# LayerNorm tail of a hybrid decoder layer: all norms on VectorE, the half-filled token tile first in the last column block, one thread per store

## The chip, the cores and the metric

The kernel runs on one core of a Trainium2 chip. The core has five engines that work side by side, each through its own instruction stream: TensorE (PE, matrix products into PSUM), VectorE (DVE), ScalarE (ACT), GpSimd (POOL) and SyncE (SP, which here issues every DMA). The metric is the device time of one execution in microseconds (us), the median of several runs. The profile is of one execution; its "span" is the time from the first to the last recorded instruction of the core.

## The reference, cut to what matters

One layer of a hybrid decoder step: a combined input projection, an RWKV-7 branch and a retention branch, an output projection, and a post-norm. It is done for 16 + 512 tokens of a new sequence and for 64 tokens of eight running sequences, all with 2048 features in float32. The change touches only the end:

```
h = jnp.einsum('btc,cd->btd', jnp.concatenate([o_a, o_b], axis=-1), w_out)
y = _layer_norm(ALPHA * x + h, ln_g, ln_b)
# _layer_norm: (x - mean) * rsqrt(var + 1e-5) * g + b, over the 2048 features of a token
```

The 512 prompt tokens and the 64 sample tokens are 576 rows of output: four tiles of 128 tokens (t = 0 to 3) and one of 64 (t = 4, the half-filled tile).

## The kernel before, in words

**The order of the work.** No engine's instruction stream is written out by hand. A class `Order` records the work as Python generators ("jobs"); each has a priority (`od.start(name, generator, priority)`, a small number goes first). While the main loop issues matmuls, `pump` puts in what the jobs have ready; when the main loop must wait, or has ended, `force` issues the job operation that can start first by the planner's own clock, with a penalty of `FIRST` = 200 per priority step once the matmuls are through. `od.call` defers a piece of Python until the operations ahead of it in the job are issued. What results is one fixed stream per engine. Each stream runs in order: an instruction whose inputs are not there holds up all that stand behind it on its engine. Since every operation passes through helpers, all DVE, ACT and POOL instructions carry line L363 in the profile, the matmuls L386 and the DMAs L403.

**The output projection.** The 2048 output columns are cut into four blocks of 512 (n = 0 to 3), and the 2048 inputs into 16 chunks of 128 (ki). A "cell" (n, t) is one 128 x 512 tile of the product, built in one of eight PSUM banks in turn (`obank`). Products are made from values split into a high and a low part: three matmuls per chunk for t < 4 and two for t = 4, whose matmul with the 64 low rows of the activations fills the upper half of the same bank. A weight chunk is loaded by DMA, and ACT and DVE split it into `wh` and `wl` (`gen_split`). For n = 3 the last ten chunks are held in SBUF (`HELD`): the tile that comes first in the order takes them as they come, and the other tiles follow, one whole tile after the other. In the kernel before, that order is t = 0, 1, 2, 3, 4.

**After a cell** (`gen_cell`): DVE adds ALPHA * x (loaded by `gen_xin` into one of three buffers, in the order of the cells) to the bank and writes `hh`, part of the tile named RW in the profile; for t = 4 a second DVE operation adds the upper half of the bank. Then `bn_stats` of the 512 columns. After the last cell of a token tile, `gen_stat` makes mean and variance (`bn_aggr`, tile SHT) and POOL makes rstd = (var + 1e-5)^-0.5 in two operations on one column.

**The norm** (`gen_norm`) of a token tile goes over four pieces of 512 columns. A string `SHARE` has a letter for each piece, four per token tile. For "g" (t = 0 to 2, and columns 0 to 1023 of t = 3) there are three steps on three engines: ACT computes x * rstd + nm, with nm = -mean * rstd made by DVE in one small operation; DVE multiplies by ln_g; POOL adds ln_b. For "d" (the rest of t = 3, all of t = 4) there are two DVE operations: (x - mean) * ln_g, and (that) * rstd + ln_b. Each piece's store to DRAM is issued by the same job, behind the piece's last step.

Of the kernel before, what the change touches and what calls it, by code (L numbers as in the profile page):

```python
# [12 lines left out]
ACTF = mybir.ActivationFunctionType  # L13
ALU = mybir.AluOpType
# [25 lines left out]
NPRIO = 1  # L40
OPRIO = 1
FIRST = 200.0
SHARE = "ggggggggggggggdddddd"
LATE = 5
EARLY = 14
BACKLOG = {0: 4000.0, 1: 1000.0, 2: 500.0, 3: 300.0, 4: 100.0}
# [360 lines left out]
def kernel(ctx, tc, x_prompt, x_sample, state_rwkv, state_shift, state_ret, meta_tokens, w_in, w_out,  # L407
# [3 lines left out]
    od = Order()  # L411
    V, A, G = (Engine(e, k, od) for e, k in ((nc.vector, "DVE"), (nc.scalar, "ACT"), (nc.gpsimd, "POOL")))
    T = TensorEngine(nc.tensor, od)
    mm = T.matmul
    S = Dma(nc.sync, "SP", od)
    S2 = Dma(nc.scalar, "AQ", od)
    until, mark, stage = od.until, od.mark, od.stage
# [40 lines left out]
    NM = sht[:, 120:125]  # L458
    RSTD = sht[:, 135:140]
    MV = sht[:, 125:135].rearrange("p (a b) -> p a b", b=2)  # L460
# [94 lines left out]
    def act(out, in_, func=ACTF.Copy, scale=1.0, bias=0.0):  # L555
        A.activation(out=out, in_=in_, func=func, scale=scale, bias=bias)

    def tt(out, a, b, op=ALU.mult, e=None):
        (e or V).tensor_tensor(out=out, in0=a, in1=b, op=op)

    def stt(out, a, s, b, o0=ALU.mult, o1=ALU.mult, e=None):
        (e or V).scalar_tensor_tensor(out=out, in0=a, scalar=s, in1=b, op0=o0, op1=o1)

    def ts(out, a, s1, s2=None, o0=ALU.mult, o1=ALU.add, e=None):
        if s2 is None:
            (e or V).tensor_scalar(out=out, in0=a, scalar1=s1, scalar2=None, op0=o0)
        else:
            (e or V).tensor_scalar(out=out, in0=a, scalar1=s1, scalar2=s2, op0=o0, op1=o1)
# [432 lines left out]
    def span(u, half):  # L1001

        if half:
            return H0, H1
        t0 = {"A": 14 * (u[2] in "rg"), "B": 16 * (u[2] in "qg"), "L": 0}[u[0]]
        return t0, H0 - t0
# [74 lines left out]
    chunks = []  # L1081
    events = []
# [8 lines left out]
    korder = [i for p in range(NPAIR) for i in ((p, 8 + p) if p < NPAIR - 1 else (8 + p, p))]  # L1091
    KO = len(korder)
    tiles = range(5)
    cells = [(n, t) for n in range(4) for t in tiles]
    j_in = len(chunks)
    for i in range(EARLY):
        events.append(("out", len(chunks), 0, i, (0, 1)))
        chunks.append(("out", korder[i], 0))
    for n in range(4):
        for i in range(KO):  # L1100
            events.append(("out", len(chunks), n, i, (2, 3, 4) if n == 0 and i < EARLY else tiles))
            chunks.append(("out", korder[i], n))
    j_one = j_in + EARLY + KO
    last = {ev[1]: e for e, ev in enumerate(events)}
# [48 lines left out]
    with tc.manual_schedule():  # L1153
# [78 lines left out]
        hh = RW[:, 0:10240].rearrange("p (t n) -> p t n", t=5)  # L1232
        lng = RW[:, 10240:12288]
        lnb = RW[:, 12288:14336]
        xin = [RW[:, 14336 + 512 * i:14336 + 512 * i + 512] for i in range(3)]
        obank = [(sq, pj[0], pj[1], r0, r1, m0, m1, ob)[i % 8] for i in range(len(cells))]
# [47 lines left out]
        def gen_stat(t):  # L1284
            rows = trows(t)
            mv = MV[0:rows, t, :]
            V.bn_aggr(out=mv, in_=ST6[0:rows, t].rearrange("p a b -> p (a b)"))
            rs = RSTD[0:rows, t:t + 1]
            ts(rs, mv[:, 1:2], 1.0, 1e-5, e=G)
            tt(rs, rs, NEGH[0:rows, 0:1], ALU.pow, e=G)  # L1290
            nm = NM[0:rows, t:t + 1]
            if set(SHARE[4 * t:4 * t + 4]) != {"d"}:
                stt(nm, mv[:, 0:1], -1.0, rs)
            od.call(lambda: od.start(f"N{t}", gen_norm(t), NPRIO))
            yield

        def gen_norm(t):
            rows = trows(t)
            rs, nm, mu = RSTD[0:rows, t:t + 1], NM[0:rows, t:t + 1], MV[0:rows, t, 0:1]
            dst = y_prompt[0, 128 * t:128 * t + 128, :] if t < 4 else xsamp_y  # L1300
            for n, step in ((0, 0), (1, 0), (0, 1), (2, 0), (1, 1), (0, 2), (3, 0), (2, 1), (1, 2), (3, 1), (2, 2), (3, 2)):
                sl = slice(512 * n, 512 * n + 512)
                hw = hh[0:rows, t, sl]
                who = SHARE[4 * t + n]
                if who == "d":
                    if step == 0:
                        stt(hw, hw, mu, lng[0:rows, sl], ALU.subtract, ALU.mult)
                    elif step == 2:
                        stt(hw, hw, rs, lnb[0:rows, sl], ALU.mult, ALU.add)
                elif step == 0:  # L1310
                    act(hw, hw, ACTF.Identity, rs, nm)
                elif step == 1:
                    tt(hw, hw, lng[0:rows, sl])
                else:
                    tt(hw, hw, lnb[0:rows, sl], ALU.add, e=G if who == "g" else V)
                if step == 2:
                    S.dma_start(out=dst[:, sl], in_=hw)
            yield

        xsamp_y = y_sample.rearrange("b t d -> (b t) d")  # L1320
# [24 lines left out]
        late = []  # L1345
        for e, ev in enumerate(events):
            stage["event"] = e
            j = ev[1]
            if ev[0] == "in":
                _, j, u, half, q, ui = ev  # L1350
                kind, p, s = u
                if half == 0 and q == 0:
                    if kind == "A" and s == "k":
                        od.start(f"A{p}", gen_a(p), 1)
                    if kind == "B" and s == "q":
                        od.start(f"B{p}", gen_b(p), 3)
                if q == 0 and ui:
                    od.ensure("evac", 2 * ui - 1 + half)
                if ui == 0 and half == 1 and q == 0:
                    od.ensure("x", 99)  # L1360
                od.ensure("split", j + 1)
                t0, n = span(u, half)
                b, jb = pj[half], part[j]
                for kk in range(4):
                    kt = 4 * q + kk
                    w = slice(128 * kk, 128 * kk + 128)
                    for i, (a_, x_) in enumerate(((WH[jb], xh), (WH[jb], xl), (WL[jb], xh))):
                        mm(b[:, :n], a_[:, w], x_[:, kt, t0:t0 + n], start=(kt == 0 and i == 0), stop=(kt == 15 and i == 2))
                        if kk == 3 and i == 2:
                            stage["event"] = e + 1  # L1370
                            if q == 3:
                                stage["proj"] = 2 * ui + half + 1
                        od.pump()
            else:
                _, j, n, ki, some = ev
                od.ensure("o", ki + 1)
                if ki == 0:
                    if n == 0 and 4 in some:
                        od.ensure(f"B{NPAIR-1}", 99)
                        od.ensure("shift", 99)  # L1380
                    if n:
                        od.ensure(f"F{NPAIR-1}", 99)
                        od.ensure("cell", 5 * n + 5 - 8)
                od.ensure("split", j + 1)
                work = [(t, ki, part[j]) for t in some]
                if n == 3 and ki >= KO - HELD:
                    late += work[1:]
                    work = work[:1]
                    if ki == KO - 1:
                        work += sorted(late, key=lambda w: w[0])  # L1390
                for iw, (t, k_, jb) in enumerate(work):
                    b = obank[5 * n + t]
                    if k_ == 0 and b in pj:
                        od.ensure("evac", 2 * len(units) - 1 + pj.index(b))
                    tok = slice(128 * t, 128 * t + 128)
                    if t < 4:
                        todo = [(b, xo[:, k_, tok], WH[jb]), (b, xl[:, k_, tok], WH[jb]), (b, xo[:, k_, tok], WL[jb])]
                    else:
                        todo = [(b, xo[:, k_, tok], WH[jb]), (b[0:64], xo[:, k_, 512:576], WL[jb])]
                        if k_ == KO - 1:  # L1400
                            todo.reverse()
                    for i, (b_, x_, w_) in enumerate(todo):
                        end = i == len(todo) - 1
                        mm(b_, x_, w_, start=(k_ == 0 and i == 0), stop=(k_ == KO - 1 and end))
                        if k_ == KO - 1 and end:
                            stage["out"] = 5 * n + t + 1
                        if iw == len(work) - 1 and end:
                            stage["event"] = e + 1
                        od.pump()
# [41 lines left out]
```

## Time and profile before

| | us |
|---|---|
| median of the runs (lowest to highest) | 1382.36 (1382.06 to 1383.02) |
| the profiled execution | 1382.55 |
| its span | 1380.8 |
| PE busy | 1331.4 (96%) |
| DVE busy | 884.0 (64%) |
| ACT busy | 644.7 (47%) |
| POOL busy | 72.5 (5%) |

The profiled execution took 1.75 us more than its span and 0.19 us more than the median. The mean granted TensorE clock was 0.991. Busy shares are means over the whole span; the change lies in the last 60 us, so what is read are the rows of that stretch: start, duration, engine, operation, output<-inputs, and in brackets the idle time before it and what ended it. The last matmul of the kernel starts at 1356.81 us; the remaining 24 us of the span have no TensorE work.

### The profile page before, as it was taken

The numbers are of one execution on the slowest core, as the hardware profiler recorded it, in microseconds if no ns is written. First come the engines' busy times: TensorE is split into PE (matmuls) and PEld (weight loads), VectorE is DVE, ScalarE is ACT, GpSimd is POOL, SyncE is SP. The second block draws the span as 40 slices with busy tenths as digits, with TensorE's granted clock in tenths as the row PEclk, the third lists the DMA queues.
The fourth block names the chain that finished last, engine by engine and source line by source line (L and its number), as shares of the span: only waits on it lengthen the run. The fifth ranks groups of instructions, "written<-read, shape, count | busy, mean of one in ns | idle before, by whom it ended". The sixth has DMA issues, their size and how long they took to land.

```text
span 1380.8 us, 26964 instructions
## 1 busy us (share of the span) xinstructions
PE 1331.4 (96%) x10392; PEld 1230.1 (89%) x10392; DVE 884.0 (64%) x2158; ACT 644.7 (47%) x1519; POOL 72.5 (5%) x131
## 2 busy tenths in 40 slices
PE   7999999999999999999999999999999999999993
PEld 6999899989998999899989998999899987777782
DVE  5774677566766676667666765676567658624347
ACT  4534564366336633663356435643564366512121
POOL 0000000000000000000000000100010001000024
PEclk9999999999999999999999999999999999999997
DMA  7343224322432243224322432243224347654313
GB/s 238 87 109 90 69 74 118 94 66 72 118 87 73 66 123 85 75 65 120 84 81 64 118 80 81 63 118 85 80 62 120 88 138 214 195 166 117 98 48 122
DMA packets 232342, 139.79 MB, mean 101 GB/s; under 512 B 58668, under 2 KB 212102, under 8 KB 231238
## 3 DMA queue, kind: packets, MB, share of 16 engines
q1 hardware_dynamic: 232214, 138.08, 35.3%
q8 instruction: 81, 1.33, 0.4%
q14 instruction: 47, 0.39, 0.1%
HBM read 119.30 MB, written 18.74 MB: 100 GB/s over the span
## 4 chain that ended last, share of the span: by engine, by line
PE 81%; DVE 9%; ACT 6%; issue 3%; DMA 0%; POOL 0%; DVEq 0%; SPq 0%; ACTq 0%; POOLq 0%
PE bank L386 77%; DVE RW L363 5%; PE bank L392 4%; DVE wl L363 1%; ACT RW L363 1%; ACT SF L363 1%; ACT XH L363 1%; DVE MOM L363 1%; ACT RT L363 1%; ACT RHS L363 1%; ACT wh L363 1%; DVE RT L363 1%; ACT RSv L363 1%; DVE SHT L363 1%; DVE XL L363 0%
## 5 line engine op out<-in xcount | busy, mean ns | idle before, releaser
L386 PE MATMUL bank<-XH,wl 128*128 128x320 f32 (+3 forms) x2080 | 634.0, 305 | 2.1 <-DVE wl L363 2.1
L386 PE MATMUL bank<-XL,wh 128*128 128x320 f32 (+3 forms) x2080 | 629.1, 302 | 0.0
L386 PE MATMUL bank<-XH,wh 128*128 128x320 f32 (+3 forms) x2080 | 627.5, 302 | 1.2 <-ACT wh L363 1.2
L386 PEld LDWEIGHTS bank<-XL,wh 128*128 128x128 f32 x2080 | 391.9, 188 | 7.9 <-issue 6.3
L386 PEld LDWEIGHTS bank<-XH,wl 128*128 128x128 f32 x2080 | 392.9, 189 | 6.0 <-DVE wl L363 3.6
L386 PEld LDWEIGHTS bank<-XH,wh 128*128 128x128 f32 x2080 | 392.8, 189 | 3.0 <-ACT wh L363 1.4
L363 DVE TENSOR_TENSOR wl<-raw,wh 128x512 fp32r<-128x512 f32 x292 | 201.4, 691 | 203.0 <-ACT wh L363 200.1
L363 ACT ACTIVATE wh<-raw 128x512 fp32r<-128x512 f32 x292 | 184.1, 631 | 205.3 <-PE bank L386 178.6
L363 DVE TENSOR_TENSOR RW<-RW 120x84 f32<-120x84 f32 (+27 forms) x558 | 149.9, 272 | 19.5 <-ACT RW L363 4.0
L386 PE MATMUL bank<-RW 32*32 32x32 f32 (+6 forms) x1904 | 146.8, 242 | 2.9 <-DVE RW L363 2.0
L386 PEld LDWEIGHTS bank<-RW 32*32 32x32 f32 (+4 forms) x1904 | 108.9, 145 | 28.0 <-DVE RW L363 9.0
L363 ACT ACTIVATE RW<-bank 128x512 f32<-128x512 f32 (+8 forms) x218 | 93.2, 438 | 47.2 <-PE bank L392 33.3
L363 ACT ACTIVATE RT<-bank 64x320 f32<-64x320 f32 (+9 forms) x122 | 47.7, 398 | 126.4 <-DVE RT L363 102.7
L363 ACT ACTIVATE SF<-RW,FT 64x64 f32<-64x64 f32 x144 | 49.7, 345 | 71.1 <-DVE RW L363 69.2
L386 PE MATMUL bank<-more,XH 128*128 128x512 f32 (+1 forms) x250 | 75.9, 395 | 0.0
L363 ACT ACTIVATE RW<-bank,OMM 128x272 f32<-128x272 f32 (+1 forms) x66 | 33.2, 502 | 68.9 <-PE bank L386 67.4
L386 PE MATMUL bank<-wh,XH 128*128 128x512 f32 x157 | 62.0, 396 | 0.0
L392 PE MATMUL bank<-CT,RW 128*128 128x128 f32 (+2 forms) x348 | 53.7, 282 | 8.2 <-DMA RW<-in_x_prompt_dram 7.5
L386 PE MATMUL bank<-wl,XH 128*128 128x512 f32 (+1 forms) x157 | 61.6, 394 | 0.0
L386 PEld LDWEIGHTS bank<-more,XH 128*128 128x128 f32 (+1 forms) x250 | 45.6, 183 | 12.4
L363 DVE TENSOR_TENSOR RW<-bank,N 64x128 f32<-64x128 f32 x80 | 22.5, 282 | 46.8 <-PE bank L386 45.7
L392 PEld LDWEIGHTS bank<-CT,RW 128*128 128x128 f32 (+2 forms) x348 | 41.2, 139 | 10.4 <-issue 7.5
(154 smaller groups left out, 1397.3 us busy)
## 6 DMA issues: line engine op xcount, KB each, us to landing
raw<-in_w_in_dram SPq DMA_DIRECT2D x259, 256.0 KB
raw<-in_w_out_dram SPq DMA_DIRECT2D x48, 256.0 KB
CT<-in_w_out_dram SPq DMA_DIRECT2D x30, 256.0 KB
RT<-in_state_ret_dram SPq DMA_DIRECT2D x8, 512.0 KB
out_dram<-RT SPq DMA_DIRECT2D x8, 512.0 KB
RW<-in_x_prompt_dram SPq DMA_DIRECT2D x16, 256.0 KB
out_dram<-RW SPq DMA_DIRECT2D x16, 256.0 KB
RW<-o_d SPq DMA_DIRECT2D x14, 288.0 KB
```

What stands on the lines that cost most here:

```text
L363: self.order.submit(Op(self.key, self.cost(name, n, kw, psum), reads, [out], lambda: f(*args, **kw)))
L386: lambda: self.eng.matmul(out, lhsT, rhs, start=start, stop=stop), (passes, move, load, shape, tiles)))
L392: lambda: self.eng.transpose(out, in_, ident), (1, move, _cols(in_) / 1.2, shape, tiles)))
```

## The change

Three things. First, every norm is now done by DVE in two operations per piece: for each token tile the four (x - mean) * ln_g, then the four (that) * rstd + ln_b. The ACT and POOL steps, the DVE multiply and the small operation for nm are gone; POOL still makes rstd. Second, in the last column block the token tiles go in the order `TURN` = 4, 0, 1, 2, 3, so the half-filled tile is the first; banks, x loads and cells follow that order (`index` gives the place of a cell). Third, a store is no longer issued by the norm's job: as soon as a piece's last operation is issued, a job of its own with priority 0 is started for its store.

```diff
-SHARE = "ggggggggggggggdddddd"
+TURN = (4, 0, 1, 2, 3)
...
-    cells = [(n, t) for n in range(4) for t in tiles]
+    cells = [(n, t) for n in range(4) for t in (TURN if n == 3 else tiles)]
+    index = {c: i for i, c in enumerate(cells)}
...
-            events.append(("out", len(chunks), n, i, (2, 3, 4) if n == 0 and i < EARLY else tiles))
+            events.append(("out", len(chunks), n, i, (2, 3, 4) if n == 0 and i < EARLY else TURN if n == 3 else tiles))
...
-            nm = NM[0:rows, t:t + 1]
-            if set(SHARE[4 * t:4 * t + 4]) != {"d"}:
-                stt(nm, mv[:, 0:1], -1.0, rs)
             od.call(lambda: od.start(f"N{t}", gen_norm(t), NPRIO))
             yield
 
+        def gen_put(dst, src):
+            S.dma_start(out=dst, in_=src)
+            yield
+
         def gen_norm(t):
             rows = trows(t)
-            rs, nm, mu = RSTD[0:rows, t:t + 1], NM[0:rows, t:t + 1], MV[0:rows, t, 0:1]
+            rs, mu = RSTD[0:rows, t:t + 1], MV[0:rows, t, 0:1]
             dst = y_prompt[0, 128 * t:128 * t + 128, :] if t < 4 else xsamp_y
-            for n, step in ((0, 0), (1, 0), (0, 1), (2, 0), (1, 1), (0, 2), (3, 0), (2, 1), (1, 2), (3, 1), (2, 2), (3, 2)):
-                sl = slice(512 * n, 512 * n + 512)
-                hw = hh[0:rows, t, sl]
-                who = SHARE[4 * t + n]
-                if who == "d":
-                    if step == 0:
-                        stt(hw, hw, mu, lng[0:rows, sl], ALU.subtract, ALU.mult)
-                    elif step == 2:
-                        stt(hw, hw, rs, lnb[0:rows, sl], ALU.mult, ALU.add)
-                elif step == 0:
-                    act(hw, hw, ACTF.Identity, rs, nm)
-                elif step == 1:
-                    tt(hw, hw, lng[0:rows, sl])
-                else:
-                    tt(hw, hw, lnb[0:rows, sl], ALU.add, e=G if who == "g" else V)
-                if step == 2:
-                    S.dma_start(out=dst[:, sl], in_=hw)
+            cut = lambda n: slice(512 * n, 512 * n + 512)
+            for n in range(4):
+                stt(hh[0:rows, t, cut(n)], hh[0:rows, t, cut(n)], mu, lng[0:rows, cut(n)], ALU.subtract, ALU.mult)
+            for n in range(4):
+                stt(hh[0:rows, t, cut(n)], hh[0:rows, t, cut(n)], rs, lnb[0:rows, cut(n)], ALU.mult, ALU.add)
+                od.call(lambda n=n: od.start(f"W{t}{n}", gen_put(dst[:, cut(n)], hh[0:rows, t, cut(n)]), 0))
             yield
...
-                        work += sorted(late, key=lambda w: w[0])
+                        work += sorted(late, key=lambda w: TURN.index(w[0]))
...
-                    b = obank[5 * n + t]
+                    b = obank[index[n, t]]
...
-                            stage["out"] = 5 * n + t + 1
+                            stage["out"] = index[n, t] + 1
```

**DVE, from the first token tile of the last column block to the middle of the second.** Names: RW holds `hh`, ln_g and ln_b; SHT holds mean, variance and rstd; a bank is a cell's PSUM tile. Before:

```order
L363 SCALAR_TENSOR_TENSOR RW<-RW,bank_120 128x512
L363 BN_STATS SHT<-RW 128x6
L363 BN_AGGR SHT<-SHT 128x2
L363 SCALAR_TENSOR_TENSOR SHT<-SHT 128x1
L363 TENSOR_TENSOR RW<-RW 128x512 x3
L363 SCALAR_TENSOR_TENSOR RW<-RW,bank_119 128x512
```

And with the change, the same place:

```order
L363 SCALAR_TENSOR_TENSOR RW<-RW,bank_120 64x512
L363 TENSOR_TENSOR RW<-bank_120,RW 64x512
L363 BN_STATS SHT<-RW 64x6
L363 BN_AGGR SHT<-SHT 64x2
L363 SCALAR_TENSOR_TENSOR RW<-RW,SHT 64x512 x8
L363 SCALAR_TENSOR_TENSOR RW<-RW,bank_119 128x512
L363 BN_STATS SHT<-RW 128x6
L363 BN_AGGR SHT<-SHT 128x2
L363 SCALAR_TENSOR_TENSOR RW<-RW,SHT 128x512 x8
```

The 64-row tile now opens the block, and each token tile's eight norm operations stand as one run between its `BN_AGGR` and the next tile's first operation on a bank. The same four-row group with x8 then follows for t = 1, 2 and 3, and DVE's stream ends with the eight of t = 3.

**SP, the last eight DMAs of the program.** out_0 is the prompt's output, out_1 the sample's; DMAHW names are completion counters of earlier DMAs, and a row without DVE or Pool waits for nothing newer on those engines than the rows ahead of it did. Before (tiles, by their addresses: t = 4, 2, 3, 4, 3, 4, 3, 4):

```order
L403 DMA out_1_dram<-RW_110 64x512 [waits DMAHW7_49,DVE_49]
L403 DMA out_0_dram<-RW_110 128x512 [waits DMAHW0_49,Pool_49]
L403 DMA out_0_dram<-RW_110 128x512 [waits DMAHW1_49,Pool_49]
L403 DMA out_1_dram<-RW_110 64x512 [waits DMAHW2_49,DVE_49]
L403 DMA out_0_dram<-RW_110 128x512 [waits DMAHW3_49,DVE_49]
L403 DMA out_1_dram<-RW_110 64x512 [waits DMAHW4_49,DVE_49]
L403 DMA out_0_dram<-RW_110 128x512 [waits DMAHW5_49,DVE_49]
L403 DMA out_1_dram<-RW_110 64x512 [waits DMAHW6_49,DVE_49]
```

With the change, the last seven are, by their addresses, (tile, piece) (3, 0), (1, 3), (2, 2), (3, 1), (2, 3), (3, 2), (3, 3):

```order
L403 DMA out_0_dram<-RW_110 128x512 [waits DMAHW0_49,DVE_49]
L403 DMA out_0_dram<-RW_110 128x512 [waits DMAHW1_49]
L403 DMA out_0_dram<-RW_110 128x512 [waits DMAHW2_49]
L403 DMA out_0_dram<-RW_110 128x512 [waits DMAHW3_49,DVE_49]
L403 DMA out_0_dram<-RW_110 128x512 [waits DMAHW4_49]
L403 DMA out_0_dram<-RW_110 128x512 [waits DMAHW5_49,DVE_49]
L403 DMA out_0_dram<-RW_110 128x512 [waits DMAHW6_49,DVE_49]
```

The stores of the half-filled tile have moved up, and three stores of t = 1 and t = 2 stand behind the first store of t = 3, whose row waits for the fifth of t = 3's eight DVE operations. All seven are full tiles of 256 KB.

## The prediction

> **What bounds the kernel now.** I read the end of the chain of waits first, then the timeline of the last 60 us engine by engine. Up to 1357 us TensorE sets the pace and the change gives it the same matmuls, so only the end can move. The end of the chain (start, us, what):
>
> ```profile
> 1360.85 1.34 DVE RW L363 x2
> ...
> 1363.92 1.86 DVE RW L363 x4
> 1365.78 5.71 issue
> 1371.49 3.38 DVE RW L363 x5
> 1374.88 0.66 DVEq L1438
> 1375.54 1.99 DVE RW L363 x3
> ```
>
> It is DVE alone, with a hole of 5.71 us that no wait explains. The timelines of TensorE and DVE show that DVE is late well before the matmuls end:
>
> ```profile
> 1324.55 0.40 PE L386 MATMUL bank<-wh,XH 128*128 128x512 f32 x1
> ...
> 1331.29 0.39 PE L386 MATMUL bank<-wl,XH 128*128 128x512 f32 x1
> 1356.81 0.39 PE L386 MATMUL bank<-wh,XH 128*128 128x512 f32 x1
> 1331.72 0.69 DVE L363 SCALAR_TENSOR_TENSOR RW<-RW,bank 128x512 f32<-128x512 f32 x1 [5.83 <-PE bank L386]
> 1332.44 0.69 DVE L363 BATCH_NORM_STATS2 SHT<-RW 128x6 f32<-128x512 f32 x1
> 1333.17 0.26 DVE L363 BATCH_NORM_AGGREGATE SHT<-SHT 128x2 f32<-128x24 f32 x1
> 1347.01 0.68 DVE L363 SCALAR_TENSOR_TENSOR RW<-RW,bank 128x512 f32<-128x512 f32 x1
> 1355.50 0.68 DVE L363 SCALAR_TENSOR_TENSOR RW<-RW,bank 128x512 f32<-128x512 f32 x1
> 1361.52 0.67 DVE L363 SCALAR_TENSOR_TENSOR RW<-RW,bank 64x512 f32<-64x512 f32 x1
> 1362.22 0.69 DVE L363 TENSOR_TENSOR RW<-bank,RW 64x512 f32<-64x512 f32 x1
> 1362.95 0.68 DVE L363 BATCH_NORM_STATS2 SHT<-RW 64x6 f32<-64x512 f32 x1
> 1363.67 0.26 DVE L363 BATCH_NORM_AGGREGATE SHT<-SHT 64x2 f32<-64x24 f32 x1
> ```
>
> The first two rows are the first and last of the 30 matmuls of t = 0: (1331.29 - 1324.55) / 29 = 0.2324 us apart, 6.97 us per full tile. DVE takes up t = 2 at 1347.01 and t = 3 at 1355.50, 8.49 us later. So from there DVE falls behind, and t = 4, whose last matmul starts at 1356.81, is taken up at 1361.52. Why DVE needs so long stands in POOL's rows beside its own:
>
> ```profile
> 1364.01 1.10 POOL L363 TENSOR_SCALAR SHT<-SHT 64x1 f32<-64x1 f32 x1 [4.66 <-DVE SHT L363]
> 1365.20 0.94 POOL L363 TENSOR_TENSOR SHT<-SHT,NEGH 64x1 f32<-64x1 f32 x1
> 1366.11 4.91 POOL L363 TENSOR_TENSOR RW<-RW 128x512 f32<-128x512 f32 x4
> 1365.65 5.92 DVE L363 SCALAR_TENSOR_TENSOR RW<-RW,SHT 64x512 f32<-64x512 f32 x1
> 1340.49 0.19 POOL L363 TENSOR_SCALAR SHT<-SHT 128x1 f32<-128x1 f32 x1 [0.82 <-DVE SHT L363]
> 1340.77 0.56 POOL L363 TENSOR_TENSOR SHT<-SHT,NEGH 128x1 f32<-128x1 f32 x1
> 1341.36 1.24 DVE L363 SCALAR_TENSOR_TENSOR SHT<-SHT 128x1 f32<-128x1 f32 x1 [0.95 <-POOL SHT L363]
> 1376.79 0.73 DVE L363 SCALAR_TENSOR_TENSOR RW<-RW,SHT 64x512 f32<-64x512 f32 x1
> ```
>
> One DVE operation that takes 0.73 at 1376.79 lasts 5.92 at 1365.65, just while POOL works off four ln_b additions. And POOL's two one-column operations, 0.19 and 0.56 with DVE idle, last 1.10 and 0.94 beside a busy DVE. The two engines shut each other out. The hole of 5.71 us in the chain is POOL's work.
>
> **The change part by part.** Times are those of the profiled execution (span 1380.8, its own time 1382.55); I move the median, 1382.36, by the difference in span.
>
> *Removed:* ACT's 14 operations and POOL's 14 additions, with the hole. DVE loses 14 multiplies and four small operations and gets 28 two-input operations more. The price of one, back to back with POOL silent, is the last row of the chain, 1.99 / 3 = 0.663. Beside running matmuls I expect the same: the like operation of 592 columns averages 0.87, against 0.73 + 80 columns at 0.73 / 512 = 0.84 worked out:
>
> ```profile
> L363 DVE SCALAR_TENSOR_TENSOR RW<-RW,VEC 128x592 f32<-128x592 f32 x25 | 21.7, 870 | 0.9
> ```
>
> *DVE per token tile.* Bank operation 0.72 (1332.44 - 1331.72), bn_stats 0.73, bn_aggr 0.26 with a gap of 0.04, eight norm operations 5.30: 7.05. For t = 4, two bank operations (0.70 + 0.73), bn_stats 0.72, 0.30 and 5.30: 7.75.
>
> *The wait for rstd, and what POOL still takes.* The first four operations need only the mean; the fifth waits for POOL, 4 x 0.663 = 2.65 us after the first. Beside a busy DVE POOL needed 1366.14 - 1363.93 = 2.21 us from the end of bn_aggr, so the wait is covered, with 0.4 us to spare. But POOL's power operation kept DVE out from 1365.65 to at least 1366.14: 0.49 us. The nearest row either way:
>
> ```profile
> 1152.71 3.02 POOL L363 TENSOR_TENSOR MOM<-MOM,NEGH 128x5 f32<-128x5 f32 x1
> 1155.17 0.69 DVE L363 TENSOR_TENSOR wl<-raw,wh 128x512 fp32r<-128x512 f32 x1
> ```
>
> Here a power operation lasts 3.02 while DVE's operation runs its usual 0.69 beside its end: DVE loses nothing and POOL waits. So the lower bound is 0. The upper bound is that POOL gets in only when DVE stops before the fifth operation: 0.19 + 0.09 + 0.56 + 0.03 = 0.87 (gaps from the rows of 1340). I take 0.49, the same operation in the same place; 7.54 and 8.24 per tile.
>
> The Trainium skill, "SBUF — State Buffer", section "SBUF: two separate sides", says that a DVE operation with two SBUF inputs and a GpSimd operation that reads SBUF exclude each other, and that whoever starts first holds the ports for its whole instruction. The rows of 1365.65 agree in kind, the row of 1155.17 does not: there DVE ran beside the power operation's end. By the rule the sum would be 1376.4 (the variant is among the rivals), by the rows 1375.1.
>
> *The half-filled tile first.* It has 20 matmuls where t = 0 had 30, so the first cell is ready earlier: 1324.55 + 19 x 0.2324 + 0.43 (from 1331.29 to 1331.72) = 1329.40, against 1331.72. Its weights must be split in time: the last split ends at 1325.88 and is needed near 1324.55 + 18 x 0.2324 = 1328.73.
>
> ```profile
> 1325.19 0.69 DVE L363 TENSOR_TENSOR wl<-raw,wh 128x512 fp32r<-128x512 f32 x1 [2.53 <-ACT wh L363]
> 1339.40 0.47 SPq L403 DMA_DIRECT2D RW<-in_x_sample_dram  x1
> ```
>
> The last x load waits for a buffer that the first operation of t = 0 frees, and stands on SP behind the first store of t = 4, which waits for that tile's fifth norm operation. Before, the last x load was issued at 1339.40; now I expect 1338.4, for use near 1360. That is hidden; if not, the third tile's start would move by what is missing.
>
> *DVE's end.* After t = 4 each tile's matmuls are through 0.57 us per tile faster than DVE (6.97 against 7.54), and t = 0 is complete at 1329.40 + 6.97 = 1336.37 while DVE ends t = 4 at 1337.64. So DVE runs without a gap: 1329.40 + 8.24 + 4 x 7.54 = 1367.80, and the last operation, which lasts 0.73 and not 0.663, ends at 1367.87. Before it was 1377.52: 9.65 us gained.
>
> *The stores.* Before, the last operation ended 3.28 us ahead of the span's end. That tail grows, by the order of SP's stream: the store of (3, 0) is followed by six more of 256 KB, three of them of t = 1 and t = 2, which were ready long before but stand behind it.
>
> ```profile
> 1367.39 0.33 SPq L403 DMA_DIRECT2D out_dram<-RW  x1
> 1368.20:1368.95 0.75, 0.00 (x0) 0.00 (x0) 0.75 (x1) 0.00 (x0) 0.75 (x2) 0.50 0.89 347
> 1372.92 5.11 SPq L403 DMA_DIRECT2D out_dram<-RW  x8
> 1374.00:1379.40 5.40, 0.00 (x0) 0.00 (x0) 3.53 (x6) 0.00 (x0) 0.00 (x0) 0.50 0.89 291
> 1379.40:1380.80 1.40, 0.00 (x0) 0.00 (x0) 0.00 (x0) 0.00 (x0) 0.00 (x0) 0.50 0.00 1
> ```
>
> (The windows' last two figures are the DMA share and GB/s.) A lone full store, issued at 1367.39, moves within 1368.20 to 1368.95 at 347 GB/s; the eight stores of the old tail, half of them 64 rows, moved at 291 from 1374.00, 1.08 after the first issue; the span ended 1.40 after the last byte. With E for the end of DVE's last operation, (3, 0) can be issued at E - 3 x 0.663 + 0.04 = E - 1.95, and moves from E - 1.0 (0.95 later, between 0.81 and 1.08). Seven times 262,144 bytes at 347 GB/s are 5.29 us: E + 4.29, and 1.40 more is E + 5.69. Bounds: 3.28 if the backlog costs nothing, and at 291 GB/s 6.31 for the bytes, E + 6.71. I take 5.69, since all seven are full tiles.
>
> *Sum:* span 1367.87 + 5.69 = 1373.56, 7.24 less than 1380.8. The median: 1382.36 - 7.24 = **1375.1 us**.
>
> **The rivals.** *POOL costs DVE nothing* (row 1155.17): 5 x 0.49 = 2.45 off, 1372.7. Against it: there DVE waited for nothing in between, here it met the power operation at 1365.65.
>
> *POOL's two operations stop DVE for their length or until the fifth operation:* 0.19 + 0.56 = 0.75 gives 5 x 0.26 = 1.3 more, 1376.4; 0.87 gives 5 x 0.38 = 1.9 more, 1377.0. For it: the 1.10 of the first one, which missed an opening of DVE. This first variant is what the whole-instruction rule of the Trainium skill's page named above would make of it.
>
> *The tail stays short:* 3.28 for 5.69, 1372.7. It would need seven stores to move in some 2.9 us, 640 GB/s, which no window shows.
>
> *Slower: POOL holds DVE out in each tile as at 1365.65.* If that hole hung on the power operation and not on the additions, each tile would lose 5.92 - 0.73 = 5.19 instead of 0.49: 5 x 4.7 = 23.5 more, 1398.6. It decides from 0.49 + (1382.36 - 1375.1) / 5 = 1.94 us per tile on. Against it: the hole ends with the fourth addition, 1366.11 + 4.91 = 1371.02, and the 1.24 of row 1341.36 is one addition long.
>
> *The change does not do what it says:* TensorE stalls at the shorter first tile for as long as DVE starts earlier, 1331.72 - 1329.40 = 2.32, and rstd comes a microsecond late in each tile, 5.0: 1375.1 + 7.3 = 1382.4. The splits' rows speak against it.
>
> **How the numbers follow.** Forecast 0.52, POOL free 0.17, POOL longer 0.20, short tail 0.05, slower 0.03, no gain 0.03. What a measurement of this kernel can tell from no change is about 0.2%, 2.8 us: 1379.6 to 1385.1. The first four cases lie below it: faster 0.94, same 0.03, slower 0.03. The range takes in POOL's two bounds (1372.7 and 1377.0), and the store rate of 291 GB/s with the longer wait, 1377.0 + 1.0 = 1378.0; below, a little of POOL free together with a shorter tail: 1372.0 to 1378.0.
>
> **What would show it.** In the changed profile: the first bank operation of 64 rows near 1329.4; the next tiles' bank operations 7.5 apart (7.05 if POOL is free, 7.8 to 7.9 if it holds DVE longer); no DVE norm operation above about 1.3; the last DVE operation ending near 1367.9; the DMA engines at about 340 GB/s for some 5 us after that operation's end minus 1, and the span ending 5 to 6 us behind it. Wrong would be a DVE idle for a bank or an x load after 1337, a norm operation of several microseconds, or a tail near 3.3.

## The result, and the profile after

| | before | after |
|---|---|---|
| median of the runs (lowest to highest), us | 1382.69 (1382.06 to 1383.52) | 1372.26 (1372.02 to 1373.04) |
| the profiled execution | 1382.55 | 1372.47 |
| its span | 1380.8 | 1370.7 |
| DVE's last operation ends | 1377.52 | 1365.13 |
| from there to the span's end | 3.28 | 5.57 |

The kernel before was run once more beside the change, so its median here is 1382.69 where the forecast started from 1382.36. The ratio is 0.9925, with an interval of 0.9908 to 0.9942. The forecast was 1375.1 us with a range of 1372.0 to 1378.0. DVE ends 12.39 us earlier, the tail behind it is 2.29 longer, and the difference, 10.10, is the gain of the span.

The head of the page of the changed kernel:

```profile
span 1370.7 us, 26934 instructions
PE 1330.4 (97%) x10392; PEld 1229.4 (90%) x10392; DVE 881.7 (64%) x2168; ACT 634.3 (46%) x1505; POOL 55.9 (4%) x117
```

ACT lost 14 operations and POOL 14. DVE has ten more and still about the same busy time (881.7 against 884.0). The sums do not explain the gain; its place is the end of the chain of waits (start, us, what), which before held "5.71 issue":

```profile
1356.02 2.68 DVE RW L363 x4
1358.71 0.71 DVE SHT L363
1359.74 0.81 DVE RW L363 x2
1361.08 2.07 DVE RW L363 x3
1363.81 1.32 DVE RW L363 x2
```

No hole of that size is left: behind 1350 the longest "issue" piece of the chain is 0.52, and DVE's rows show it busy meanwhile. DVE's timeline from the first cell of the last column block (tile t = 4, then t = 0 to 3):

```profile
1328.98 0.68 DVE L363 SCALAR_TENSOR_TENSOR RW<-RW,bank 64x512 f32<-64x512 f32 x1 [3.48 <-PE bank L386]
...
1331.43 5.38 DVE L363 SCALAR_TENSOR_TENSOR RW<-RW,SHT 64x512 f32<-64x512 f32 x8
1336.84 0.69 DVE L363 SCALAR_TENSOR_TENSOR RW<-RW,bank 128x512 f32<-128x512 f32 x1
...
1338.59 5.39 DVE L363 SCALAR_TENSOR_TENSOR RW<-RW,SHT 128x512 f32<-128x512 f32 x8
1343.90 0.68 DVE L363 SCALAR_TENSOR_TENSOR RW<-RW,bank 128x512 f32<-128x512 f32 x1
...
1350.95 0.68 DVE L363 SCALAR_TENSOR_TENSOR RW<-RW,bank 128x512 f32<-128x512 f32 x1
...
1358.01 0.68 DVE L363 SCALAR_TENSOR_TENSOR RW<-RW,bank 128x512 f32<-128x512 f32 x1
...
1359.74 5.39 DVE L363 SCALAR_TENSOR_TENSOR RW<-RW,SHT 128x512 f32<-128x512 f32 x8
```

Only the first row has idle time before it. From there on DVE runs without a gap; the full tiles follow each other by (1358.01 - 1336.84) / 3 = 7.06 us, where before two of them were 8.49 apart. Not all of those 8.49 were POOL's additions. In the kernel before, DVE stood idle in that tile for 0.95 until POOL had rstd and for 0.89 until ACT had the first piece (the figures in brackets), and both waits are gone with the change:

```profile
1349.66 1.24 DVE L363 SCALAR_TENSOR_TENSOR SHT<-SHT 128x1 f32<-128x1 f32 x1 [0.95 <-POOL SHT L363]
1351.78 3.80 DVE L363 TENSOR_TENSOR RW<-RW 128x512 f32<-128x512 f32 x4 [0.89 <-ACT RW L363]
```

With the change, eight norm operations take 5.38 or 5.39 in every tile. POOL's rows beside them, for t = 0:

```profile
1338.65 0.75 POOL L363 TENSOR_SCALAR SHT<-SHT 128x1 f32<-128x1 f32 x1 [5.39 <-DVE SHT L363]
1339.48 0.94 POOL L363 TENSOR_TENSOR SHT<-SHT,NEGH 128x1 f32<-128x1 f32 x1
```

These took 0.19 and 0.56 with DVE idle. Now they take 0.75 and 0.94: POOL pays, and DVE's eight operations are as long as without it. In t = 4 it is the same; the power operation there and the DVE operation that starts while it runs:

```profile
1332.31 0.94 POOL L363 TENSOR_TENSOR SHT<-SHT,NEGH 64x1 f32<-64x1 f32 x1
1332.76 0.74 DVE L363 SCALAR_TENSOR_TENSOR RW<-RW,SHT 64x512 f32<-64x512 f32 x1
```

For t = 0, rstd is there at 1340.42; the fifth norm operation needs it at 1338.59 + 2.65 = 1341.24.

The tail, in SP's timeline (the last x load, the store of (3, 0), the last store) and in windows of the whole core, whose last two figures are the DMA share and GB/s:

```profile
1337.56 0.33 SPq L403 DMA_DIRECT2D RW<-in_x_prompt_dram  x1
...
1363.17 0.33 SPq L403 DMA_DIRECT2D out_dram<-RW  x1
...
1366.36 0.59 SPq L403 DMA_DIRECT2D out_dram<-RW  x1
```

```profile
1363.90:1364.10 0.20, 0.00 (x0) 0.00 (x0) 0.20 (x1) 0.00 (x0) 0.00 (x0) 0.50 0.44 174
...
1364.50:1369.00 4.50, 0.00 (x0) 0.00 (x0) 0.63 (x1) 0.00 (x0) 0.00 (x0) 0.50 1.00 366
...
1369.20:1369.40 0.20, 0.00 (x0) 0.00 (x0) 0.00 (x0) 0.00 (x0) 0.00 (x0) 0.50 0.01 0
```

All 16 DMA engines are full for 4.5 us, at 366 GB/s, most of it after DVE has ended. That is the backlog of seven stores.

### The profile page after: what moved, and what is told of

It reads as the page before. It is cut to its first block, busy times and chain, and to the rows that moved or that the text cites. A ratio compares the mean times of both kernels' runs of the same rounds, so it can differ in the third digit from the quotient of the medians.

```text
span 1370.7 us, 26934 instructions
## 1 busy us (share of the span) xinstructions
PE 1330.4 (97%) x10392; PEld 1229.4 (90%) x10392; DVE 881.7 (64%) x2168; ACT 634.3 (46%) x1505; POOL 55.9 (4%) x117
## 4 chain that ended last, share of the span: by engine, by line
PE 80%; DVE 10%; ACT 6%; issue 3%; DMA 0%; POOL 0%; DVEq 0%; SPq 0%; ACTq 0%
PE bank L386 77%; DVE RW L363 6%; PE bank L392 4%; DVE wl L363 1%; ACT SF L363 1%; ACT XH L363 1%; DVE MOM L363 1%; ACT RHS L363 1%; ACT RT L363 1%; ACT RW L363 1%; ACT wh L363 1%; DVE RT L363 1%; ACT RSv L363 1%; DMA RW<-in_x_prompt_dram 0%; DVE XL L363 0%
## 5 line engine op out<-in xcount | busy, mean ns | idle before, releaser
L363 DVE TENSOR_TENSOR RW<-RW 120x84 f32<-120x84 f32 (+26 forms) x544 | 137.7, 256 | 16.6 <-DMA RW<-lt_d 2.7
```

Of the source, the lines that this page charges most:

```text
L363: self.order.submit(Op(self.key, self.cost(name, n, kw, psum), reads, [out], lambda: f(*args, **kw)))
```

## The experiments

Where an expectation names 5.3 us for the tail of the changed kernel, its rows say 5.57 (1370.7 - 1365.13). "Tail" is the time from the end of DVE's last operation to the end of the span. A bank operation is DVE's first operation on a finished cell. Medians are set against those of the kernel before in the same series; DVE's end, span and tail are those of one profiled execution.

| kernel | median, us | before | ratio (interval) | DVE's end | span | tail |
|---|---|---|---|---|---|---|
| order alone | 1379.60 | 1382.20 | 0.9983 (0.9974 to 0.9992) | 1373.54 | 1377.7 | 4.16 |
| norms alone | 1374.21 | 1382.20 | 0.9947 (0.9934 to 0.9959) | 1368.38 | 1372.2 | 3.82 |
| both, stores in the norm's job | 1373.25 | 1382.20 | 0.9935 (0.9922 to 0.9949) | 1366.39 | 1371.2 | 4.81 |
| the change once more | 1372.84 | 1382.68 | 0.9928 (0.9916 to 0.9940) | 1365.56 | 1371.1 | 5.54 |
| the change, stores freed | 1368.95 | 1382.20 | 0.9910 (0.9897 to 0.9924) | 1365.42 | 1368.7 | 3.28 |
| + one POOL addition of 512 per tile | 1378.14 | 1382.68 | 0.9968 (0.9954 to 0.9981) | 1371.09 | 1376.6 | 5.51 |
| + one POOL addition of 64 | 1373.25 | 1382.68 | 0.9933 (0.9920 to 0.9947) | 1365.96 | 1371.4 | 5.44 |
| + one POOL copy of 512 | 1374.11 | 1382.68 | 0.9942 (0.9928 to 0.9956) | 1367.76 | 1373.3 | 5.54 |
| + four POOL additions of 512 | 1393.04 | 1382.63 | 1.0075 (1.0046 to 1.0104) | 1386.69 | 1391.2 | 4.51 |

### Which part of the change brings what

**All norms by DVE, in the old order of tiles.** The kernel before with one line changed:

```diff
-SHARE = "ggggggggggggggdddddd"
+SHARE = "dddddddddddddddddddd"
```

> The kernel before with the letter d for all twenty pieces and nothing else: all norms by DVE in two operations, tiles in the order 0 to 4, stores in the norm's job. Theory (the gain is DVE freed from POOL's additions; the tile order brings 2.3 us of DVE time and the store backlog takes most of it back): DVE runs without a gap from 1331.7, 7.05 us per full tile and 7.75 for t = 4, its last operation ends near 1367.7, the tail is about 3.5, the time 1372.6 to 1373.2. Rival (the half-filled tile first is what brings the gain): most of the 10 us are missing, 1379 or more.

8.0 us of gain (1382.20 - 1374.21): 1.0 above the upper end of what was expected, and far from the rival's 1379. Its DVE timeline shows what the expectation left out:

```profile
1337.90 0.69 DVE L363 SCALAR_TENSOR_TENSOR RW<-RW,bank 128x512 f32<-128x512 f32 x1 [1.15 <-PE bank L386]
...
1344.87 0.69 DVE L363 SCALAR_TENSOR_TENSOR RW<-RW,bank 128x512 f32<-128x512 f32 x1 [0.49 <-PE bank L386]
...
1359.76 8.62 DVE L363 SCALAR_TENSOR_TENSOR RW<-RW,SHT 128x512 f32<-128x512 f32 x13
```

The planner placed two norm operations of a tile behind the next tile's bank operation. DVE waits 1.15 and 0.49 for TensorE there, with work queued behind the waiting instruction, and does that work at the end: 13 norm operations where 8 belong to the last tile.

**The order of the tiles alone.** The kernel before with `TURN`, `index` and the places that use them; norms and stores as they were.

> The kernel before with the tile order 4, 0, 1, 2, 3 in the last column block and nothing else: ACT, DVE and POOL share the norms as before. Theory: DVE starts 2.3 us earlier, but still needs 8.3 to 8.5 us per tile of the shared kind and is held up by POOL's additions at the end, and the store backlog adds some 2 us to the tail: 1379 to 1382, at most 3 us of gain. Rival (the order brings the gain): 1374 or less.

2.6 us: the expectation held. DVE and POOL still alternate at the end:

```profile
1370.13 1.75 DVE L364 SCALAR_TENSOR_TENSOR RW<-RW,SHT 128x512 f32<-128x512 f32 x1
1371.80 1.75 DVE L364 SCALAR_TENSOR_TENSOR RW<-RW,SHT 128x512 f32<-128x512 f32 x1
1369.69 1.64 POOL L364 TENSOR_TENSOR RW<-RW 128x512 f32<-128x512 f32 x1 [1.29 <-DVE RW L364]
1371.29 1.70 POOL L364 TENSOR_TENSOR RW<-RW 128x512 f32<-128x512 f32 x1
```

Each of the two DVE operations, 0.73 or 0.74 undisturbed, takes 1.75 beside one of the two additions.

**Without the threads for the stores.** The changed kernel, with the store again part of the norm's job:

```diff
-                od.call(lambda n=n: od.start(f"W{t}{n}", gen_put(dst[:, cut(n)], hh[0:rows, t, cut(n)]), 0))
+                S.dma_start(out=dst[:, cut(n)], in_=hh[0:rows, t, cut(n)])
```

> The changed kernel with each store issued again by the norm's own job, behind its operation. Theory: DVE's operations stand in another order (the last three of t = 2 move behind the statistics of t = 3) but their sum is the same, and SP's last seven stores are the same seven: 1372.3 within 0.5 us, the threads alone bring nothing. Rival (without threads the norm's operations wait for the stores ahead of them): DVE has gaps, or the last stores pile up more; 1374 or more.

The middle, 1373.25, is 0.95 above what was expected; the runs lie between 1371.22 and 1373.38. The ratios overlap with those of the change, so what the threads bring is not told apart from nothing. What the trace shows is a trade. Its DVE timeline:

```profile
1343.31 0.69 DVE L363 SCALAR_TENSOR_TENSOR RW<-RW,bank 128x512 f32<-128x512 f32 x1 [0.51 <-PE bank L386]
...
1359.01 7.38 DVE L363 SCALAR_TENSOR_TENSOR RW<-RW,SHT 128x512 f32<-128x512 f32 x11
```

DVE waits for banks again (0.47 and 0.51), has 11 norm operations at the end and stops 1.26 us later than in the change (1366.39 - 1365.13); the tail is 0.76 shorter (4.81 against 5.57). The last seven stores still move in one go, but the first of them is issued at 1363.77, 2.62 ahead of DVE's end, where in the change it was 1.96.

**The backlog of stores.** Where does it come from? The planner describes an access to DRAM by the stretch from its first to its last address. The four column pieces of a token tile interleave row by row, so their stretches overlap, and the planner makes each store wait, by its clock, for the landing of the one before it, although they share no byte. This kernel hides the destination from the planner, in `gen_put`:

```diff
-            S.dma_start(out=dst, in_=src)
+            od.submit(Op("SP", 480.0, [src], [], lambda: nc.sync.dma_start(out=dst, in_=src), 4.0 * 512 * src.shape[0]))
```

> The changed kernel, but the planner is no longer told that two stores of one token tile touch the same stretch of DRAM, so SP's stream has each tile's four stores right behind one another; every other engine's stream is the same. Theory (the three late stores of t = 1 and t = 2 make the tail): DVE's last operation ends 5.3 us ahead of the span's end in the changed kernel; here 3.2 to 3.5, since the last four stores start 0.66 us apart and move in 0.74 each; time about 2.0 us below the changed kernel's 1372.3, that is 1370.2. Rival (the tail is the fixed price of a burst of full stores): 5.3 again, 1372.3.

DVE works as in the change, and the tail falls back to 3.28; the median, 1368.95, is below what was expected (the profiled execution, 1370.44, is the slowest of the four). All four runs lie below every run of the change, whose lowest is 1371.28, although the intervals of the ratios overlap. The last DVE row, and windows of the end:

```profile
1360.03 5.39 DVE L363 SCALAR_TENSOR_TENSOR RW<-RW,SHT 128x512 f32<-128x512 f32 x8
```

```profile
1363.50:1367.50 4.00, 0.00 (x0) 0.00 (x0) 1.92 (x3) 0.00 (x0) 0.00 (x0) 0.50 0.68 262
1367.50:1368.70 1.20, 0.00 (x0) 0.00 (x0) 0.00 (x0) 0.00 (x0) 0.00 (x0) 0.50 0.00 0
```

From 1363.5 on 4.00 x 262 = 1.05 MB move, four stores of 262,144 bytes: those of t = 3 alone. In the change it was seven. This is the fastest kernel of the study, 13.25 us below the kernel before.

### What POOL costs DVE

The forecast charged 0.49 us per tile for POOL's two one-column operations; the trace showed nothing. These runs add idle POOL work to the changed kernel, behind rstd in `gen_stat`; its result is not used, and the output stays the same.

**The change once more**, as the standard for this series:

> The changed kernel itself, unaltered, beside the next three on one chip, as their base line: 1372.3, its last DVE operation 5.3 us ahead of the span's end, all norm operations of DVE 0.66 apart.

1372.84: the same as the first time, within its runs (1371.28 to 1373.36).

**One addition of 512 columns per tile:**

```diff
+            tt(RAW[0], lng[:, 0:512], lnb[:, 0:512], ALU.add, e=G)
```

> The changed kernel with one POOL addition of 128x512 (ln_g + ln_b into a buffer that nobody reads any more) behind rstd in each of the five token tiles, an idle task beside the norms. Theory (a two-input addition of POOL holds DVE out for nearly its length, 1.0 to 1.25, as in the kernel before; the one-column operations cost nothing): in each tile one or two of DVE's norm operations last 1.0 to 1.3 longer, DVE's end is 5 to 6.3 us later, the time 1377.3 to 1378.6. Rival (what held DVE out before was the power operation in that place, or the wait for rstd): 1372.3.

**One of 64 columns** (`0:64` on all three):

> The same with an addition of 64 columns instead of 512. Theory (POOL holds DVE out in proportion to the columns, which is why one column costs nothing): 0.15 to 0.35 per tile, 1373.0 to 1374.0. Rival (every POOL operation that follows close behind another holds DVE out by a fixed half microsecond or more, whatever its size): 1374.8 or more.

**One copy of 512 columns:**

```diff
+            G.tensor_copy(RAW[0], lng[:, 0:512])
```

> The same with a POOL copy of 512 columns, one input in SBUF instead of two. If any POOL operation that reads SBUF shuts out DVE's two-input operations for its whole length (the section of the Trainium skill's page SBUF — State Buffer that the prediction names says so): the copy's full length per tile, an estimate of 1.5 from 0.38 for 128 columns, 5 x 1.5 = 7.5: 1379.8. If only its second input is what collides: 1372.3.

The timelines at the same place, each with the POOL operation, the DVE operation ahead and the one that is held: first the addition of 512, then that of 64, then the copy.

```profile
1350.36 1.43 POOL L363 TENSOR_TENSOR raw<-RW 128x512 f32<-128x512 f32 x1
1349.90 0.75 DVE L363 SCALAR_TENSOR_TENSOR RW<-RW,SHT 128x512 f32<-128x512 f32 x1
1350.56 1.78 DVE L363 SCALAR_TENSOR_TENSOR RW<-RW,SHT 128x512 f32<-128x512 f32 x1
```

```profile
1347.62 0.74 DVE L363 SCALAR_TENSOR_TENSOR RW<-RW,SHT 128x512 f32<-128x512 f32 x1
1348.08 0.46 POOL L363 TENSOR_TENSOR raw<-RW 128x64 f32<-128x64 f32 x1
1348.28 0.81 DVE L363 SCALAR_TENSOR_TENSOR RW<-RW,SHT 128x512 f32<-128x512 f32 x1
```

```profile
1348.55 0.75 DVE L363 SCALAR_TENSOR_TENSOR RW<-RW,SHT 128x512 f32<-128x512 f32 x1
1348.99 0.77 POOL L363 COPY raw<-RW 128x512 f32<-128x512 f32 x1
1349.21 1.10 DVE L363 SCALAR_TENSOR_TENSOR RW<-RW,SHT 128x512 f32<-128x512 f32 x1
```

In the 128-row tiles the one DVE operation that starts after POOL's becomes longer, and the others keep their length. (In the 64-row tile the copy makes two of them longer, to 1.09 each, and the first of these starts 0.45 ahead of the copy.) The addition of 512 begins at 1350.36, 0.20 before the DVE operation that it holds, while the DVE operation ahead runs until 1350.65. The loss of a full tile, from the distance of the bank operations in each DVE timeline; 7.06 is the change's own, which equals the 7.05 worked out without POOL:

| POOL operation | its length | bank operations of t = 0 and t = 3 start | a third of it | DVE loses |
|---|---|---|---|---|
| 1 column, two operations (the change) | 0.75, 0.94 | 1336.84, 1358.01 | 7.06 | 0.00 |
| addition, 64 columns | 0.46 | 1337.42, 1358.78 | 7.12 | 0.06 |
| copy, 512 columns | 0.77 | 1338.06, 1360.28 | 7.41 | 0.35 |
| addition, 512 columns | 1.43 | 1338.73, 1362.97 | 8.08 | 1.02 |

The expectation on the 512 addition held for the full tiles (the 64-row tile lost 1.56). That on 64 columns was near in time (1373.25 within 1373.0 to 1374.0) but too high per tile; the rival of a fixed price per POOL operation falls. On the copy both theories missed: it was assumed to last 1.5, lasted 0.77, and cost less than half of that. So a POOL operation has no fixed price. What DVE loses follows how long POOL's row goes on after the end of the DVE operation ahead: 0.18 for the addition of 64 (1348.54 - 1348.36), 0.46 for the copy (1349.76 - 1349.30), 1.14 for the addition of 512 (1351.79 - 1350.65). The loss is 0.11 or 0.12 less each time.

The Trainium skill, "SBUF — State Buffer", section "SBUF: two separate sides", says that the engine that begins first keeps the shared ports for its whole instruction and the other is fully blocked. Beside full tiles the additions and the copy agree in kind, if the part of POOL's row that overlaps the DVE operation ahead is a wait for the ports, which no record shows directly. Two things do not agree. The one-column power operation of t = 0 ends at 1340.42, 0.42 after the second DVE norm operation has ended (the first two take from 1338.59 to 1340.00), and costs 0.00. And in the 64-row tile the copy lengthens a DVE operation that started ahead of it.

**Why one hole of 5.92 before?** With one addition costing 1.02, four should have cost 4.1 in four pieces, and the kernel before lost 5.19 in one operation. Two runs with four additions per tile:

```diff
+            for _ in range(4):
+                tt(RAW[0], lng[:, 0:512], lnb[:, 0:512], ALU.add, e=G)
```

> The changed kernel with four idle additions on POOL behind rstd of each token tile, 512 columns each, all ready at once (their inputs are ln_g and ln_b, their result is not used, so the output stays the same). Question: why did one DVE operation of the kernel before last 5.92 us at 1365.65, through four additions, when a single addition in each tile cost 1.03? Theory A, a waiting DVE operation is let in after each addition: in each tile four norm operations of about 1.78 us, 4 x 1.03 = 4.1 us more per tile, bank operations 11.2 apart, about 20.6 us more in all, time near 1393. Theory B, additions that stand ready one behind the other keep DVE out until the last is through: in each tile one norm operation of 0.74 + 4 x 1.24 - some 0.3 = 5.4 to 5.9 us and the others unchanged, 4.7 to 5.2 us more per tile, bank operations 11.8 to 12.3 apart, time 1396 to 1398.5.

Theory A came out: 1393.04 where it said 1393, and bank operations 11.22 and 11.08 apart for t = 0 to 2 where it said 11.2. Then the same with additions in place, on the buffers in turn, as those before were:

```diff
+            for q in range(4):
+                tt(RAW[q % 3], RAW[q % 3], lnb[:, 512 * q:512 * q + 512], ALU.add, e=G)
```

> As the kernel with four idle additions per token tile, but each addition is in place, on another buffer and another piece of ln_b, as the four additions of the kernel before at 1366.11 were (those stood 1.22 us apart and let no DVE operation in; the four that read ln_g and ln_b and wrote elsewhere let one in after each and stood 1.68 apart). Theory A, being in place makes no difference: additions 1.6 to 1.7 us apart, no norm operation above 2.3 us, time near 1393. Theory B, additions in place that are ready keep DVE out until the last: additions about 1.22 us apart, in each tile one norm operation of 5.4 to 5.9 us, time 1396 to 1398.5.

One run, 1392.23 beside 1382.97 of the kernel before; its span is 1390.2. Neither theory holds for all tiles. First t = 4, with its 64 rows, then t = 0, with 128:

```profile
1332.87 6.04 DVE L363 SCALAR_TENSOR_TENSOR RW<-RW,SHT 64x512 f32<-64x512 f32 x1
1333.32 1.29 POOL L363 TENSOR_TENSOR raw<-raw,RW 128x512 f32<-128x512 f32 x1
1334.58 1.28 POOL L363 TENSOR_TENSOR raw<-raw,RW 128x512 f32<-128x512 f32 x1
1335.83 1.28 POOL L363 TENSOR_TENSOR raw<-raw,RW 128x512 f32<-128x512 f32 x1
1337.07 1.29 POOL L363 TENSOR_TENSOR raw<-raw,RW 128x512 f32<-128x512 f32 x1
...
1345.99 1.78 DVE L363 SCALAR_TENSOR_TENSOR RW<-RW,SHT 128x512 f32<-128x512 f32 x1
1345.80 1.43 POOL L363 TENSOR_TENSOR raw<-raw,RW 128x512 f32<-128x512 f32 x1
1347.19 1.73 POOL L363 TENSOR_TENSOR raw<-raw,RW 128x512 f32<-128x512 f32 x1
```

The hole is there again, in the 64-row tile alone: 6.04 us, with POOL's additions 1.25 apart. Beside the 128-row operations of the same run the two engines take turns. With the additions that wrote one buffer (the run before), the 64-row operation was held through one addition only:

```profile
1333.61 2.29 DVE L363 SCALAR_TENSOR_TENSOR RW<-RW,SHT 64x512 f32<-64x512 f32 x1
1334.06 1.29 POOL L363 TENSOR_TENSOR raw<-RW 128x512 f32<-128x512 f32 x1
1335.43 1.63 POOL L363 TENSOR_TENSOR raw<-RW 128x512 f32<-128x512 f32 x1
```

There 0.08 us lie between the first addition's end (1335.35) and the second's start; in place, each addition begins before the record of the one ahead has ended. So in these runs the long hole came only where both were there: a DVE operation on 64 rows, and additions that follow each other without that gap. It does not hang on the place of the 64-row tile, which was the last in the kernel before and is the first here. Whether it is the gap itself, being in place or the change of buffers was not separated, and why 64 rows differ from 128 stays open.

## Why the prediction was right, and where it was off

The forecast was 2.84 us too high (1375.1 against 1372.26), and the span as much (1373.56 against 1370.7). By its steps:

- **What bounds the end.** Right: DVE alone, with POOL's additions beside it. The prediction put no price on DVE's waits for rstd and for ACT in the kernel before, 0.95 and 0.89 in the tile of 1347.01; its sum, built from the new operations, did not need one. With POOL's large operations gone the eight norm operations of a tile take 5.39 in every tile, and one addition put back into each tile returns 5.3 us (1378.14 - 1372.84).
- **DVE per tile.** 7.05 and 7.75 without POOL's part were worked out; 7.06 and 1336.84 - 1328.98 = 7.86 came. The price of 0.663 for a norm operation beside running matmuls held; no dearer row was seen.
- **What POOL still takes: the step that failed.** The term of 0.49 per tile, 2.45 in the sum, measured 0.00. The rival "POOL costs DVE nothing", with its 1372.7 and a chance of 0.17, is what happened. The misreading was of the row at 1365.65. I took the time from that operation's start to the first addition as lost to the power operation. The changed kernel has the same overlap in t = 4, without additions behind it (the rows of 1332.31 and 1332.76 above): the power operation goes on for 0.49 beside the DVE operation (1333.25 - 1332.76), just as at 1365.65, and the DVE operation lasts its usual 0.74. So the power operation took nothing there, and the long row came from the additions. The run with additions in place repeats that row: the held operation starts at 1332.87, the first addition 0.45 later at 1333.32, and the operation ends 0.55 after the last addition (1338.91 against 1338.36). The row of 1155.17, which the prediction quoted as the lower bound, was the right neighbour.
- **The wait for rstd.** Covered, as said: 0.8 to spare where 0.4 was worked out.
- **The half-filled tile first.** First bank operation 1329.40 worked out; 1328.98 in this trace and 1329.41 in the second one of the same kernel, so right within the scatter. The last x load was issued at 1337.56 (forecast 1338.4), and no DVE row after 1337 waits for one.
- **DVE's end.** 1367.87 forecast, 1365.13 measured. Of the 2.74, 2.45 are POOL's term and 0.42 the earlier start; 0.13 go the other way, most of it the 7.86.
- **The stores.** Right in mechanism and nearly in size: 5.69 forecast, 5.57 measured, 5.44 to 5.54 in four other runs with one POOL operation or none added. The store of (3, 0) was issued at 1363.17, which is E - 1.96 for E - 1.95. The bytes took 5.0 us and not 5.29, since they moved at 366 GB/s and not 347; the wait behind the last byte was some 1.6 us and not 1.40. The rival of a short tail needed seven stores in 2.9 us and did not come; the tail became short only when three of the seven were moved ahead.
- **The slower rivals.** A hole as at 1365.65 in each tile was set aside because it hung on the additions. The runs with four additions bear that out, and narrow it: the hole came with the additions in place, and beside a 64-row operation alone.

What the forecast left unsaid is how its parts share the gain: about 8 us for the norms, 2.6 for the order alone, together 9 without the threads. With all norms on DVE the order still ends DVE 1.99 us earlier (1368.38 against 1366.39), but the tail grows by 0.99 (3.82 against 4.81), so half of it is lost to the stores (the two kernels also differ in the order of the eight operations of a tile).

## What to carry to other kernels

Before a neighbour's small operation is given a price, look at what the other engine's operations last while it waits: here POOL's own rows grew (0.19 to 0.75, 0.56 to 0.94) and DVE's did not. Large two-input POOL operations beside DVE operations of the same kind saved nothing here: taking them off POOL, and doing their work on DVE, made DVE end earlier. And when DVE no longer sets the end, look at the order of the last stores: three stores that were ready long before, but stood behind one that was not, cost 2.3 us of tail.

## What the runs showed of the hardware that was not expected

- POOL's one-column operations fit between DVE's two-input operations at no cost to DVE (0.00 per tile in ten operations), while they themselves last 0.75 and 0.94.
- DVE's loss beside a POOL operation is not the length of POOL's row: 0.06 for an addition of 64 columns (0.46 long), 0.35 for a copy of 512 (0.77), 1.02 for an addition of 512 (1.43). Beside 128-row operations it is 0.11 or 0.12 less than what POOL's row lasts beyond the end of the DVE operation ahead.
- The same POOL operations cost more beside 64-row DVE operations than beside 128-row ones. From the first to the second bank row of t = 4 and t = 0, the time against the change's 7.86 grew by 0.71 with the copy (8.57), which made two DVE operations longer by 0.35 each, and by 1.56 with the addition of 512 (9.42). Four additions in place held one 64-row operation for 6.04 us and took turns with 128-row ones.
- A backlog of full 256 KB stores moved at 366 GB/s, where a single one before showed 347.
